# Small inputs in one load, a threshold search shared by two engines, and final norms in five steps: the Hyena and mixture-of-experts trunk on one core

## The chip, the core and the metric

The kernel runs on one core of a Trainium2 chip. The metric is device time of one execution in microseconds, as the median over timed runs. One more execution was recorded by the hardware profiler; the rows below are of that one. Engines are named as in the profile: PE does matrix multiplies, DVE, ACT and POOL work elementwise, SP only issues transfers (DMAs), and ACT and POOL can issue them too.

## The reference, cut to what matters

One layer over 2048 tokens of width 1024. A modulation vector comes from `silu(c) @ mod_w + mod_b`, the tokens are normalised and modulated, a Hyena mixer follows (input projection, a centred 3-tap convolution, two long convolutions whose filters are computed from sines, output projection), then a norm, a second modulation, an expert-choice mixture of experts and a last norm.

```python
x = x + grid_pos_embed(rows, D_MODEL)
m_l = split(silu(c) @ mod_w[i] + mod_b[i], 6)
hl = layer_norm(x) * (1.0 + m_l[1]) + m_l[0]
yl = hyena(hl, ...)              # filters: sin(freq * (z @ f_w1 + f_b1)), twice more with f_w2, f_b2
x = ln_affine(ALPHA * x + (1.0 + m_l[2]) * yl, ln_g[i, 0], ln_b[i, 0])
hl = layer_norm(x) * (1.0 + m_l[4]) + m_l[3]
aff = softmax(hl @ w_router)                       # 2048 x 16
gate, idx = top_k(aff.T, 256)                      # each of 16 experts takes its 256 best tokens
he = silu(xe @ w1) * (xe @ w3)                     # xe = hl[idx], 256 x 1024; w1, w3: 1024 x 2048
ye = (he @ w2) * gate                              # w2: 2048 x 1024
x = ln_affine(ALPHA * x + (1.0 + m_l[5]) * scatter_add(ye), ln_g[i, 1], ln_b[i, 1])
```

## The kernel before, in words

Matrix products of 32-bit floats are made of halves: a tile is cast by ACT to a rounded high part (`wh`, `hh`, `w1h`), and DVE subtracts it from the original to give the low part (`wl`, `hl`, `w1l`). Two or three products of parts make one full product.

**Start.** Three strands run together. `early_mod` loads 16 pieces of `mod_w` (tile `mw`, five buffers, issued by SP) and multiplies them by `sg`, partly on PE, partly on DVE into `macc` (L464, L467); PE then sums over partitions into `sd` (L470), and `md` (L473) is the modulation. `filter_acts` makes the filters' sines: PE multiplies, ACT scales (`turn`, L211), DVE reduces to one turn (`kk`, L213 and L214), ACT takes the sine (L215). `side_steps` normalises the tokens in quarters of four tiles: POOL adds the position terms (L496, L497), DVE takes statistics (`bst`, `stat`), `rstd_steps` turns variance into 1/sqrt (`lva`, `lsq`, `r`, `nb`; L383 to L392), ACT applies it (L506), PE transposes, ACT applies `md` (`ht`, L526), and the input projection (`ip`) begins. Small parameters come in transfers of their own: `cs` and `mb` by SP, `fb` in six by ACT (L193 to L195), `prm` in three by ACT (L593 to L595), the latter gathered four bytes at a time. A scheduler sets the order of instructions on each engine here.

**Route.** After the output projection the router's logits `lg` go through a softmax. `phase_route` finds each expert's 256th largest score by a search over the bits of its value, two bits in a step, 15 steps: DVE counts scores at or above three candidates (three instructions at L1320, with a sum kept by each), PE adds the counts over the partitions of an expert (`cp`, L1322), DVE counts how many candidates have 256 or more (`ge`, L1338) and makes the next candidates (`cand`, L1342; the partial threshold `thr` at L1328 and the next bases at L1335). Meanwhile the first expert's weights are split: ACT casts and POOL subtracts, six tensors of 128x2048 (`split(raws, nc.gpsimd)`, L1401). `route(0)` then gathers the first expert's 256 tokens by an indirect transfer and transposes them in four steps through one buffer, `tp`.

**Experts.** Sixteen experts in turn, each in eight chunks of 256 hidden columns, each chunk in two halves. A half is `project` (w1 and w3 products), `hidden` (silu times the other, `u`, then `hh` and `hl`) and `back` (product with w2 into `acc`, one half later). Weights of a later chunk are cast by ACT (L1400) and split by DVE (L1401); SP issues their loads in order.

**The last three experts** are written in an order by hand, 16 steps (`n`) of one half each. Between their steps `settle` does the last norm of the tokens, 256 at a time. It is a generator of which one step runs in each half: load; nothing; statistics and, right behind them, 1/sqrt by three Newton steps in tiny POOL operations (L1565 to L1577); then ACT's scaling of `xs` (L1580) and POOL's `gb` multiply and add (L1581, L1582) and the store. `plan` says at which step of which expert a settle starts, ten in all here. The buffers `free` of the settles belong to the pair that also holds the experts' gathered tokens, so `route(e + 1)` writes its `xs` (L1484) into a buffer that a settle used.

## Time and profile before

| | us |
|---|---|
| median of 3 runs | 4089.68 (4086.54 to 4090.18) |
| the profiled execution, its own time | 4085.04 |
| its span, first to last instruction | 4083.2 |
| PE busy | 3833.0 (94%) |
| DVE / ACT / POOL busy | 2789.9 / 1940.8 / 1040.3 |
| from the end of the search to the experts' first product | 1827.80 to 1846.77 |

The span is the time that the rows of the trace add up to; 1.84 us lie around it. The profiled execution is 4.64 us below the median of the runs shown.

### The profile page before, as it was taken

What the parts mean: (1) busy time and instruction counts of PE and PEld (TensorE: products, weight loads), DVE (VectorE), ACT (ScalarE), POOL (GpSimd) and SP (SyncE); (2) the same over time, 40 slices, a digit from 0 to 9 for tenths busy, and PEclk for the clock granted to TensorE, in tenths of its full rate; (3) what the DMA queues carried; (4) which work ended last, traced back from release to release, by engine and by line L of the source; (5) the groups of instructions that cost most, each with busy time, mean ns of one, the idle gap of its engine ahead of it and who ended that gap; (6) DMA issues with size and microseconds to landing.
All of it is one profiled execution on the core that took longest, in us unless ns stands there. A gap on an engine that the chain in (4) does not pass through costs nothing.

```text
span 4083.2 us, 52931 instructions
## 1 busy us (share of the span) xinstructions
PE 3833.0 (94%) x19839; PEld 3171.7 (78%) x19839; DVE 2789.9 (68%) x4017; ACT 1940.8 (48%) x2845; POOL 1040.3 (25%) x1092
## 2 busy tenths in 40 slices
PE   4899999999999989939999999999999999999997
PEld 3666766777777877827888888888888888888896
DVE  5777876776877877785666666666666666656766
ACT  3544543333777651114555555555555555544443
POOL 2355552212455442220000000000000000014635
PEclk8999999999999999969999999999999999999999
DMA  6355656667999986445666665666566656656764
GB/s 201 113 175 173 179 172 210 221 205 227 268 283 278 294 251 203 136 162 167 196 193 209 206 196 188 214 204 195 188 215 203 195 189 213 203 176 221 238 228 159
DMA packets 620796, 831.73 MB, mean 204 GB/s; under 512 B 56627, under 2 KB 506947, under 8 KB 618236
## 3 DMA queue, kind: packets, MB, share of 16 engines
q1 hardware_dynamic: 545594, 661.93, 50.8%
q0 software_dynamic: 57088, 163.48, 13.7%
q10 hardware_dynamic: 17858, 2.95, 0.5%
q8 instruction: 156, 2.56, 0.3%
q14 instruction: 100, 0.82, 0.1%
HBM read 643.82 MB, written 150.75 MB: 195 GB/s over the span
## 4 chain that ended last, share of the span: by engine, by line
PE 75%; DVE 9%; issue 5%; DMA 4%; POOL 3%; ACT 3%; SPq 0%; ACTq 0%; POOLq 0%; DVEq 0%
PE ab L1502 19%; PE ab L1503 10%; PE acc L175 5%; PE acc L176 5%; PE acc L177 5%; PE ip L175 3%; PE ip L177 3%; PE ip L176 3%; PE sp L335 2%; PE xp L854 2%; PE ap L889 2%; PE xp L872 2%; PE op L175 1%; PE op L177 1%; PE op L176 1%
## 5 line engine op out<-in xcount | busy, mean ns | idle before, releaser
L1502 PE MATMUL ab<-xs,w3h 128*128 128x512 f32 x1664 | 600.6, 399 | 0.0
L1502 PE MATMUL ab<-xs,w1h 128*128 128x512 f32 x1664 | 598.2, 399 | 0.0
L1401 DVE TENSOR_TENSOR w2l<-w2r,w2h 128x2048 fp32r<-128x2048 f32 x126 | 297.6, 2362 | 267.0 <-ACT w2h L1400 266.9
L1503 PE MATMUL ab<-xs,w3l 128*128 128x256 f32 x1664 | 468.2, 281 | 0.0
L1503 PE MATMUL ab<-xs,w1l 128*128 128x256 f32 x1664 | 466.6, 280 | 0.0
L175 PE MATMUL acc<-w2h,hh 128*128 128x512 f32 x1024 | 404.1, 395 | 14.3 <-ACT hh L170 13.8
L176 PE MATMUL acc<-w2l,hh 128*128 128x512 f32 x1024 | 402.5, 393 | 0.0
L177 PE MATMUL acc<-w2h,hl 128*128 128x512 f32 x1024 | 399.5, 391 | 0.8 <-DVE hl L171 0.8
L1502 PEld LDWEIGHTS ab<-xs,w3h 128*128 128x128 f32 x1664 | 313.0, 188 | 76.6
L1502 PEld LDWEIGHTS ab<-xs,w1h 128*128 128x128 f32 x1664 | 313.0, 188 | 72.9
L1548 POOL DMA_INDIRECT accd<-y,idx x27 | 68.5, 2535 | 1101.8 <-DVE y L1542 1095.6
L1401 DVE TENSOR_TENSOR w1l<-w1r,w1h 128x2048 fp32r<-128x2048 f32 x126 | 301.0, 2389 | 62.7 <-ACT w1h L1400 62.6
L170 ACT CAST hh<-u 128x256 fp32r<-128x256 f32 x256 | 104.1, 407 | 478.6 <-DVE u L1525 478.6
L1503 PEld LDWEIGHTS ab<-xs,w1l 128*128 128x128 f32 x1664 | 314.2, 189 | 7.1
L1506 DVE TENSOR_TENSOR u<-ab,u 128x256 f32<-128x256 f32 x416 | 174.6, 420 | 205.2 <-ACT u L1505 196.8
L1503 PEld LDWEIGHTS ab<-xs,w3l 128*128 128x128 f32 x1664 | 314.8, 189 | 0.0
L1401 DVE TENSOR_TENSOR w3l<-w3r,w3h 128x2048 fp32r<-128x2048 f32 x126 | 292.9, 2324 | 18.7 <-ACT w3h L1400 18.7
L1400 ACT CAST w2h<-w2r 128x2048 fp32r<-128x2048 f32 x128 | 244.1, 1907 | 94.7 <-PE acc L177 86.3
L1400 ACT CAST w1h<-w1r 128x2048 fp32r<-128x2048 f32 x128 | 244.5, 1910 | 80.5 <-PE ab L1502 79.0
L1400 ACT CAST w3h<-w3r 128x2048 fp32r<-128x2048 f32 x128 | 244.5, 1910 | 68.4 <-PE ab L1502 66.3
L1505 ACT COPY u<-ab 128x256 f32<-128x256 f32 x416 | 152.8, 367 | 184.9 <-PE ab L1503 184.8
L175 PE MATMUL ip<-hh,wh 128*128 128x512 f32 x576 | 237.4, 412 | 3.3 <-ACT hh L170 3.3
(399 smaller groups left out, 9114.7 us busy)
## 6 DMA issues: line engine op xcount, KB each, us to landing
w1r<-in_moe_w_dram SPq DMA_DIRECT2D x128, 1024.0 KB
w3r<-in_moe_w_dram SPq DMA_DIRECT2D x128, 1024.0 KB
w2r<-in_moe_w_dram SPq DMA_DIRECT2D x128, 1024.0 KB
fud<-ev SPq DMA_DIRECT2D x128, 256.0 KB
kr<-fud SPq DMA_DIRECT2D x64, 512.0 KB
bn<-ao POOLq DMA_DIRECT2D x248, 128.0 KB, 7.2
win<-in_c_win_dram SPq DMA_DIRECT2D x64, 256.0 KB
mw<-in_mod_w_dram SPq DMA_DIRECT2D x64, 256.0 KB
```

The source lines that it names most:

```text
L170: nc.scalar.copy(hi, raw)
L175: nc.tensor.matmul(out, lhsT=ah, rhs=bh, start=start, stop=False)
L176: nc.tensor.matmul(out, lhsT=ah, rhs=bl, start=False, stop=False)
L177: nc.tensor.matmul(out, lhsT=al, rhs=bh, start=False, stop=stop)
L335: nc.tensor.matmul(p, lhsT=s1[:, th], rhs=hb[th], start=True, stop=(n0 > 0))
L854: nc.tensor.matmul(p[:, i], lhsT=s2[:, 2 * gp + i], rhs=r[:, i], start=True, stop=True)
L1400: nc.scalar.copy(h, raw)
L1401: eng.tensor_tensor(l, raw, f_(h), OP.subtract)
L1502: nc.tensor.matmul(p, lhsT=ws[2 * j][:, k, fs], rhs=xs[:, k], start=(k == 0), stop=False)
L1503: nc.tensor.matmul(p[:, 0], lhsT=ws[2 * j + 1][:, k, fs], rhs=xs[:, k, 0], start=False, stop=(k == 7))
L1505: nc.scalar.copy(u, p[:, 1])
L1506: nc.vector.tensor_tensor(u, p[:, 0], u, OP.add)
```

## The change

Seven parts, in the order in which they run.

1. Seven small inputs are packed by the host into one array of 128x148, which one SP transfer loads into `small`; `cs`, `mb`, `fb` and `prm` become slices of it, and their eleven transfers go.
2. `rstd_steps` takes the square root straight from the variance with the epsilon as ACT's bias, without the DVE addition `lva`; the five DVE operations before `nb` become four. `kk`'s subtraction is written with another instruction, one for one.
3. At the end of the output projection the exponential's table is loaded, and the casts of the first two weight tensors are issued, ahead of the last logits.
4. In the search, DVE counts two candidates and ACT the third (a sign with a kept sum); PE adds them in two products, and `ge` compares with a row of limits `lim`.
5. POOL no longer splits the first expert's weights: DVE does, w1 and w3 of chunk 0 before the search, w2 of chunk 0 and the weights of chunk 1 behind `route(0)`.
6. `route(0, wide=True)` transposes through the projection's buffers `ab` too, and its order is now fixed by hand.
7. `settle` yields once more, between the statistics and the Newton steps, and one settle of the third-last expert starts one half later.

The diff, cut to its core:

```diff
+def host_small(x):
+
+
+    col = lambda v: np.asarray(v, dtype=np.float32).reshape(-1, 128).T
+    two = lambda v: np.concatenate([np.asarray(v, dtype=np.float32).reshape(-1, 64).T] * 2, 0)
+    return np.ascontiguousarray(np.concatenate(
+        [col(x["c"][0]), col(x["mod_b"][0, 0:2048]), col(x["hy_conv_w"][0]), col(x["hy_conv_b"][0]), col(x["hy_b_in"][0]),
+         two(x["hy_f_freq"][0]), two(x["hy_f_b1"][0]), two(x["hy_f_b2"][0])], 1))
...
     nc.scalar.dma_start(fw[0][33:66, 64:128], A["hy_f_w1"][0])
-    for s in range(2):
-        sl = slice(s * 64, s * 64 + 64)
-        nc.scalar.dma_start(fb[sl, 0:1], A["hy_f_freq"][0].unsqueeze(1))
-        nc.scalar.dma_start(fb[sl, 1:2], A["hy_f_b1"][0].unsqueeze(1))
-        nc.scalar.dma_start(fb[sl, 2:4], A["hy_f_b2"][0].rearrange("i k -> k i"))
     nc.scalar.dma_start(zt[:, 0:1024], A["c_z"][:, 0:1024])
...
-        nc.vector.tensor_tensor(kk, turn, kk, OP.subtract)
+        nc.vector.scalar_tensor_tensor(kk, kk, -1.0, turn, op0=OP.mult, op1=OP.add)
...
 def rstd_steps(nc, wk, r, nb, stat, eps, n):
 
-    va = wk.tile([128, n], F32, name="lva")
-    nc.vector.tensor_scalar(va, stat[:, :, 1], eps, None, op0=OP.add)
+    nc.scalar.activation(r, stat[:, :, 1], AF.Sqrt, bias=eps)
+    yield 1
     sq = wk.tile([128, n], F32, name="lsq")
-    nc.scalar.activation(sq, va, AF.Sqrt)
-    yield 1
-    nc.vector.reciprocal(r, sq)
-    nc.vector.tensor_tensor(sq, r, r, OP.mult)
-    nc.vector.tensor_tensor(sq, sq, va, OP.mult)
-    nc.vector.tensor_scalar(sq, sq, -0.5, 1.5, op0=OP.mult, op1=OP.add)
-    nc.vector.tensor_tensor(r, r, sq, OP.mult)
+    nc.vector.reciprocal(r, r)
+    nc.vector.scalar_tensor_tensor(sq, stat[:, :, 1], eps, r, op0=OP.add, op1=OP.mult)
+    nc.vector.scalar_tensor_tensor(sq, sq, -0.5, r, op0=OP.mult, op1=OP.mult)
+    nc.vector.scalar_tensor_tensor(r, sq, 1.5, r, op0=OP.add, op1=OP.mult)
     nc.vector.scalar_tensor_tensor(nb, stat[:, :, 0], -1.0, r, op0=OP.mult, op1=OP.mult)
...
-        prm = S.top.tile([128, 5, 24], F32, name="prm")
-        nc.scalar.dma_start(prm[:, 0:3], A["hy_conv_w"][0].rearrange("j (k p) -> p j k", p=128))
-        nc.scalar.dma_start(prm[:, 3], A["hy_conv_b"][0].rearrange("(k p) -> p k", p=128))
-        nc.scalar.dma_start(prm[:, 4], A["hy_b_in"][0].rearrange("(k p) -> p k", p=128))
+        prm = S.small[:, 24:144].rearrange("p (j k) -> p j k", j=5)
...
-            if n == 16:
+            if n == 17:
+                nc.scalar.activation(wk.tile([128, 1], F32, name="r"), ident[:, 0:1], AF.Exp)
                 next(nxt)
...
+        lim = wk.tile([128, 3], F32, name="lim")
+        nc.gpsimd.memset(lim[:, 0:2], T - CAP + 0.5)
+        nc.gpsimd.memset(lim[:, 2:3], T - 2.0 * CAP + 1.0)
...
-                cnt = wk.tile([128, 3], BF16, name="cnt", bufs=2)
-                for k in range(3):
+                cnt = wk.tile([128, 2], BF16, name="cnt", bufs=2)
+                cs = wk.tile([128, 1], BF16, name="cs", bufs=2)
+                sign = wk.tile([128, 256], BF16, name="sign")
+                with nc.allow_low_precision(reason="whole numbers of at most 256"):
+                    nc.scalar.activation(sign, v, AF.Sign, scale=-1.0, bias=cand[:, 2:3], accum_out=cs)
+                for k in range(2):
                     junk = wk.tile([128, 256], U16, name=f"junk{k}")
-                    nc.vector.tensor_scalar(junk, v, cand[:, k:k + 1], 0.0, op0=OP.is_ge, op1=OP.add, accum_out=cnt[:, k:k + 1])
+                    nc.vector.tensor_scalar(junk, v, cand[:, k:k + 1], 0.0, op0=OP.is_lt, op1=OP.add, accum_out=cnt[:, k:k + 1])
                 p = ps.tile([128, 3], F32, name="cp", bufs=2)
-                nc.tensor.matmul(p, lhsT=blkb, rhs=cnt, start=True, stop=True)
+                nc.tensor.matmul(p[:, 2:3], lhsT=blkb, rhs=cs, start=True, stop=True)
+                nc.tensor.matmul(p[:, 0:2], lhsT=blkb, rhs=cnt, start=True, stop=True)
...
-                nc.vector.tensor_scalar(ge, p, CAP - 0.5, 0.0, op0=OP.is_ge, op1=OP.add, accum_out=num)
+                nc.vector.scalar_tensor_tensor(ge, p, 1.0, lim, op0=OP.mult, op1=OP.is_le, accum_out=num)
...
+    hs = [(n, raw, wt.tile(list(raw.shape), F32R, name=n + "h"), wt.tile(list(raw.shape), F32R, name=n + "l")) for n, raw in raws]
+
+    def sub(i):
+        _, raw, h, l = hs[i]
+        nc.vector.scalar_tensor_tensor(l, raw, 1.0, f_(h), op0=OP.mult, op1=OP.subtract)
+
+    for i in range(2):
+        nc.scalar.copy(hs[i][2], hs[i][1])
+    for i in range(2):
+        sub(i)
     nc.vector.tensor_scalar(R.tri, ii, 128.0, None, op0=OP.is_gt)
     nc.vector.tensor_scalar(ii, ii, 15, None, op0=OP.bitwise_and)
     nc.vector.tensor_scalar(R.blkb, ii, 0.0, None, op0=OP.is_equal)
+    R.first = [t for h in hs for t in h[2:]]
     yield
-    R.first = []
-    for n in range(2):
-        R.first.append(split(raws, nc.gpsimd))
-        if n == 0:
-            raws = load(0, 1)
+    nc.scalar.copy(hs[2][2], hs[2][1])
+    yield
+    sub(2)
+    raws = load(0, 1)
+    R.second = split(raws[:2])
+    R.raw = raws[2:]
...
-                p = ps.tile([128, 2, 256], F32, name="tp", bufs=1)
+                p = ps.tile([128, 2, 256], F32, name="ab", bufs=3) if wide and q else ps.tile([128, 2, 256], F32, name="tp", bufs=1)
...
             for j in range(2):
                 ln_stats(nc, wk, stat, j, x[:, j])
+            yield
             va = wk.tile([128, 2], F32, name="va2")
...
-        with tc.manual_schedule():
-            for _ in route(0):
-                pass
+        first = route(0, wide=True)
+        next(first)
+        next(R.split_first)
+        next(first)
+        for _ in first:
+            pass
+        next(R.split_first)
+        order.close()
...
-        plan = {-3: {1: "xh", 3: "xl", 5: "xh"}, -2: {0: "xh", 2: "-xl", 5: "xh"}, -1: {0: "xh", 2: "-xl", 5: "xh", 7: "xl"}}
+        plan = {-3: {1: "xh", 3: "xl", 6: "xh"}, -2: {0: "xh", 2: "-xl", 5: "xh"}, -1: {0: "xh", 2: "-xl", 5: "xh", 7: "xl"}}
...
+            S.small = S.top.tile([128, 148], F32, name="small")
+            nc.sync.dma_start(S.small, A["c_small"])
```

ACT at the start of the program, from the last small filter weights to the first sines; `prm` is the convolution's and input projection's parameters, `a` a sine. Before:

```order
L201 DMA fw_121<-in_hy_f_w_dram 64x64 x2
L211 ACTIVATE turn<-sp,frq 128x512
L211 ACTIVATE turn<-g,frq 128x512
L211 ACTIVATE turn<-sp,frq 128x512
L593 DMA prm<-in_hy_conv_w_dram 128x72x1
L594 DMA prm<-in_hy_conv_b_dram 128x24x1
L595 DMA prm<-in_hy_b_in_dram 128x24x1
L215 ACTIVATE a_459<-kk 128x512 x2
L211 ACTIVATE turn<-g,frq 128x512
L211 ACTIVATE turn<-sp,frq 128x512
L215 ACTIVATE a_459<-kk 128x512
```

And after the change:

```order
L205 DMA fw_118<-in_hy_f_w_dram 64x64 x2
L215 ACTIVATE turn<-sp,frq 128x512
L215 ACTIVATE turn<-g,frq 128x512
L215 ACTIVATE turn<-sp,frq 128x512
L219 ACTIVATE a_446<-kk 128x512
L215 ACTIVATE turn<-g,frq 128x512
L219 ACTIVATE a_446<-kk 128x512
L215 ACTIVATE turn<-sp,frq 128x512
L219 ACTIVATE a_446<-kk 128x512
```

The three `prm` transfers that stood between the third `turn` and the first sine are gone, and the sines alternate with the `turn`s from there on.

DVE in one step of the search (`half` is the 16-bit half of a score that is searched, `junk` a result that nobody reads, `kc` the table of first candidates). Before:

```order
L1320 TENSOR_SCALAR junk_15099,cnt<-half_15094,kc 128x256
L1320 TENSOR_SCALAR junk_15101,cnt<-half_15094,kc 128x256
L1320 TENSOR_SCALAR junk_15103,cnt<-half_15094,kc 128x256
L1324 MEMSET thr_15097 128x1
L1326 COPY half_15093<-afp 128x256
L1335 TENSOR_SCALAR base<-kc,thr_15097 128x3
L1338 TENSOR_SCALAR ge,num<-cp 128x3
L1342 SCALAR_TENSOR_TENSOR cand<-num,base 128x3
L1320 TENSOR_SCALAR junk_15117,cnt<-half_15094,cand 128x256
```

After the change, on DVE:

```order
L1321 TENSOR_SCALAR junk_15062,cnt<-half_15054,kc 128x256
L1321 TENSOR_SCALAR junk_15064,cnt<-half_15054,kc 128x256
L1326 MEMSET thr_15057 128x1
L1328 COPY half_15053<-afp 128x256
L1337 TENSOR_SCALAR base<-kc,thr_15057 128x3
L1340 SCALAR_TENSOR_TENSOR ge,num<-cp,lim 128x3
L1344 SCALAR_TENSOR_TENSOR cand<-num,base 128x3
L1321 TENSOR_SCALAR junk_15082,cnt<-half_15054,cand 128x256
```

And on ACT, from the first weight casts to the end of the search (`sign` is the result that nobody reads, `cs` the kept sum):

```order
L1437 CAST w1h<-w1r 128x2048
L1437 CAST w3h<-w3r 128x2048
L1235 COPY lg<-rp 128x32
L1218 COPY ht<-tp 128x4x128 x2
L1228 COPY lp<-rp 128x256
L1235 COPY lg<-rp 128x32
L1285 ACTIVATE lg<-lg 128x256
L1318 ACTIVATE sign,cs<-half_15054,kc 128x256
L1318 ACTIVATE sign,cs<-half_15054,cand 128x256 x6
L1318 ACTIVATE sign,cs<-half_15053,kc 128x256
L1318 ACTIVATE sign,cs<-half_15053,cand 128x256 x7
L1445 CAST w2h<-w2r 128x2048
```

One count of three has moved to ACT; ahead of the softmax ACT now casts `w1h` and `w3h`, which stood behind it, and `w2h` comes behind the search.

DVE in the second-last expert, around one settle's statistics (`bst`, `stat` of `xs`) and the first small operations of its Newton steps (`va`, `t`, `r`). Before:

```order
L1401 TENSOR_TENSOR w1l<-w1r,w1h 128x2048
L1401 TENSOR_TENSOR w3l<-w3r,w3h 128x2048
L376 BN_STATS bst<-xs 128x6 x2
L377 BN_AGGR stat_32000<-bst 128x2
L376 BN_STATS bst<-xs 128x6 x2
L377 BN_AGGR stat_32000<-bst 128x2
L1565 TENSOR_SCALAR va_32009<-stat_32000 128x2
L1569 TENSOR_SCALAR t_32013<-va_32009 128x2
L1570 TENSOR_SCALAR r_32011<-t_32013 128x2
L1454 TENSOR_SCALAR oh<-slot,lo 128x256
L1455 SCALAR_TENSOR_TENSOR oh<-slot,hi,oh 128x256
```

After the change:

```order
L380 BN_STATS bst<-xs 128x6 x2
L381 BN_AGGR stat_32000<-bst 128x2
L380 BN_STATS bst<-xs 128x6 x2
L381 BN_AGGR stat_32000<-bst 128x2
L1469 TENSOR_SCALAR oh<-slot,lo 128x256
L1470 SCALAR_TENSOR_TENSOR oh<-slot,hi,oh 128x256
L1540 TENSOR_TENSOR u_32068<-u_32068,ab 128x256
L181 TENSOR_TENSOR hl<-u_32068,hh 128x256
L1403 TENSOR_TENSOR w2l<-w2r,w2h 128x2048
L1581 TENSOR_SCALAR va_32093<-stat_32000 128x2
L1585 TENSOR_SCALAR t_32097<-va_32093 128x2
L1586 TENSOR_SCALAR r_32095<-t_32097 128x2
```

`va` has moved from right behind the statistics to the end of the next half, behind that half's split `w2l`.

## Rows read from the trace of the kernel before

**Rows 1.** Windows: length, busy PE, PEld, DVE, ACT, POOL; PE clock, DMA share, GB/s.

```profile
0.00:115.00 115.00, 57.52 (x206) 40.77 (x207) 64.30 (x118) 48.71 (x73) 26.45 (x32) 0.82 0.62 179
115.00:680.00 565.00, 529.13 (x2356) 381.43 (x2356) 424.18 (x527) 272.77 (x468) 300.54 (x248) 0.98 0.56 169
...
1776.28:1827.80 51.52, 2.46 (x15) 1.46 (x14) 49.59 (x170) 8.64 (x5) 26.24 (x6) 0.50 0.50 162
...
1846.77:3630.00 1783.23, 1782.68 (x9470) 1520.15 (x9469) 1120.91 (x1401) 915.76 (x1198) 89.16 (x50) 1.00 0.62 197
3630.00:4063.00 433.00, 414.08 (x2871) 384.79 (x2870) 284.03 (x299) 189.33 (x194) 217.21 (x208) 0.99 0.66 219
```

**Rows 2.** Chain that ended last, the first 140 us: start, us, what.

```profile
25.60 0.80 ACTq L594
26.39 14.44 issue
...
56.78 7.00 PE sd L470 x32
```

**Rows 3.** Windows of 5 us at the start, columns as in rows 1.

```profile
40.00:45.00 5.00, 1.31 (x2) 0.80 (x3) 0.14 (x1) 1.81 (x3) 0.00 (x0) 1.00 0.55 6
```

**Rows 4.** DMA queues, first 60 us: packets, MB, share of 16 engines.

```profile
q10 hardware_dynamic: 16738, 0.72, 19.3%
```

**Rows 5.** Timeline at the start, DVE, POOL and PE: start, us, what.

```profile
44.85 0.43 DVE L213 TENSOR_SCALAR kk<-turn 128x512 f32<-128x512 f32 x1 [14.15 <-ACT turn L211]
63.80 0.24 DVE L473 SCALAR_TENSOR_TENSOR md<-sd,mb 128x8 f32<-128x8 f32 x2 [4.62 <-PE sd L470]
67.02 8.04 DVE L383 TENSOR_SCALAR lva<-stat 128x4 f32<-128x4 f32 x1
67.69 1.27 POOL L496 TENSOR_TENSOR x<-x,pr 128x512 f32<-128x512 f32 x1
80.31 0.15 DVE L392 SCALAR_TENSOR_TENSOR nb<-stat,r 128x4 f32<-128x4 f32 x1
98.53 0.79 PE L175 MATMUL ip<-x,wh 128*128 128x512 f32 x1 [7.49 <-ACT ht L526]
```

**Rows 6.** DVE groups in the search: xcount, busy us, mean ns, idle before.

```profile
L1320 DVE TENSOR_SCALAR_CACHE_REDUCE junk<-half,cand 128x256 uint16<-128x256 uint16 x39 | 16.6, 476 | 0.5
L1342 DVE SCALAR_TENSOR_TENSOR cand<-num,base 128x3 f32<-128x3 f32 x13 | 10.5, 806 | 0.5
```

**Rows 7.** Timeline of the route and the first expert.

```profile
1773.43 0.40 ACT L1287 ACTIVATE lg<-lg 128x256 f32<-128x256 f32 x1
1775.71 4.52 POOL L1401 TENSOR_TENSOR w1l<-w1r,w1h 128x2048 fp32r<-128x2048 f32 x1 [43.18 <-ACT w1h L1400]
1805.34 0.48 DVE L1320 TENSOR_SCALAR_CACHE_REDUCE junk<-half,cand 128x256 uint16<-128x256 uint16 x1
1807.29 0.48 DVE L1320 TENSOR_SCALAR_CACHE_REDUCE junk<-half,cand 128x256 uint16<-128x256 uint16 x1
1859.44 2.29 DVE L1401 TENSOR_TENSOR w1l<-w1r,w1h 128x2048 fp32r<-128x2048 f32 x1 [1.55 <-ACT w1h L1400]
```

**Rows 8.** Waits in the last experts: who for whom, total us, times, longest.

```profile
PE acc L175 <- ACT hh L170: 13.8, 8, 3.3
ACT xs L1580 <- POOL nb L1577: 38.0, 10, 6.0
ACT xs L1484 <- DMA out_dram<-xs: 4.0, 2, 2.2
SPq L1555 <- DMA out_dram<-xs: 8.9, 1, 8.9
```

**Rows 9.** Timeline of one settle in the third-last expert.

```profile
3700.74 1.27 DVE L376 BATCH_NORM_STATS2 bst<-xs 128x6 f32<-128x512 f32 x2
3703.69 1.90 DVE L1565 TENSOR_SCALAR va<-stat 128x2 f32<-128x2 f32 x1
3716.39 2.37 ACT L1580 ACTIVATE xs<-xs,nb,r 128x1024 f32<-128x1024 f32 x2 [6.02 <-POOL nb L1577]
```

More of the change, by code (lines that the diff above doesn't have):

```diff
@@ L177, in mm3, with filter_acts @@
     nc.tensor.matmul(out, lhsT=al, rhs=bh, start=False, stop=stop)
-def filter_acts(tc, A, ld, ps, afw, arv):
+def filter_acts(tc, A, fb, ld, ps, afw, arv):
     nc = tc.nc
-    fb = ld.tile([128, 4], F32, name="fb")
     zt = ld.tile([128, T], F32, name="zt")[0:66]
@@ L439, in late_mod, with early_mod @@
         yield
-def early_mod(nc, A, md, sg, ones_f, wk, ps):
-    cs = wk.tile([128, 8], F32, name="cs", bufs=1)
-    nc.sync.dma_start(cs, A["c"][0].rearrange("(k p) -> p k", p=128))
+def early_mod(nc, A, cs, mb, md, sg, ones_f, wk, ps):
     nc.scalar.activation(sg, cs, AF.Silu)
-    mb = wk.tile([128, 2, 8], F32, name="mb", bufs=1)
-    nc.sync.dma_start(mb, A["mod_b"][0, 0:2048].rearrange("(i k p) -> p i k", i=2, p=128))
     yield
@@ L503, in norm @@
         nb = wk.tile([128, 4], F32, name="nb")
-        yield from rstd_steps(nc, wk, r, nb, stat, ADALN_EPS, 4)
+        yield from rstd_steps(nc, wk, r, nb, stat, eps, 4)
         for j in range(4):
@@ L537, in side_steps @@
         pr = wk.tile([128, 512], F32, name="pr", bufs=1)
+        eps = wk.tile([128, 1], F32, name="eps", bufs=1)
+        nc.vector.memset(eps, ADALN_EPS)
         nc.gpsimd.dma_start(pr, A["c_posr"])
@@ L1287, in phase_route @@
         nc.scalar.activation(lg, lg, AF.Exp)
-        next(R.split_first)
         nc.vector.tensor_reduce(mx, lg, axis=mybir.AxisListType.X, op=OP.add)
@@ L1443, in phase_moe @@
     with ExitStack() as st:
-        with tc.manual_schedule():
-            phase_route(tc, ident, ones_f, lg, R)
+        order = st.enter_context(ExitStack())
+        order.enter_context(tc.manual_schedule())
+        phase_route(tc, ident, ones_f, lg, R)
         cst = st.enter_context(tc.tile_pool(reuse_waits="tile", name="e_cst", bufs=1))
@@ L1449, in phase_moe, with route @@
         ps = st.enter_context(tc.tile_pool(reuse_waits="tile", name="e_ps", bufs=2, space=PSUM))
-        def route(e):
+        def route(e, wide=False):
             oh = wk.tile([128, 256], F32, name="oh", bufs=1)
@@ L1588, in phase_moe @@
         nxt, pend = [], []
-        with tc.manual_schedule():
-            for _ in route(0):
-                pass
+        first = route(0, wide=True)
[6 more added lines that the diff above has]
+        order.close()
         m5 = cst.tile([128, 1024], F32, name="m5")
@@ L1605, in phase_moe @@
             for fc in range(8):
-                ws = R.first.pop(0) if R.first else R.split(R.load(e, fc))
+                if e == 0 and fc < 2:
+                    ws = (R.second + R.split(R.raw)) if fc else R.first
+                else:
+                    ws = R.split(R.load(e, fc))
                 for i in range(2):
@@ L1753, in build @@
                         tc.tile_pool(reuse_waits="tile", name="m_wk", bufs=2, side="right") as mk:
-                    mod = early_mod(nc, A, md, sg, ones_f, mk, sps)
+                    mod = early_mod(nc, A, S.small[:, 0:8], S.small[:, 8:24].rearrange("p (i k) -> p i k", i=2), md, sg, ones_f, mk, sps)
                     next(mod)
-                    acts = filter_acts(tc, A, ld, fps, afw, arv)
+                    acts = filter_acts(tc, A, S.small[:, 144:148], ld, fps, afw, arv)
                     side = side_steps(tc, A, md, ident, S, psum, h2d)
@@ L1800 @@
     given.update(host_consts())
+    given["c_small"] = host_small(given)
+    for n in ("c", "hy_conv_w", "hy_conv_b", "hy_b_in", "hy_f_freq", "hy_f_b1", "hy_f_b2"):
+        del given[n]
     for n, a in given.items():
```

4 lines of the change are left out of this document (1 added, 3 removed).

## Prediction

> **What bounds the kernel now.** Read first the windows by stage [rows 1]. From 1846.77 to 3630 PE is busy for 1782.68 of 1783.23 us: nothing that another engine does there can shorten the kernel, and whatever ends the stages before it sooner is kept. From 115 to 680 PE is busy for 529 of 565 us, so a shift that reaches the input projection is mostly handed on. Three stretches are not PE's: the first 115 us (57.52 busy), the threshold search (2.46 busy in 51.52 us, DVE 49.59) and the last three experts (414.08 of 433.00, so 18.9 us of holes). The change touches these three.
>
> Next, the start. The chain of waits [rows 2] shows ACT at L594 from 25.60, then 14.44 us under "issue", then PE's sums `sd` at 56.78. ACT issues the small `prm` transfers in the same order in which it computes sines, so DVE, which wants ACT's `turn` for `kk` at 44.85, stands idle for 14.15 us [rows 5], and DVE's multiplications of `mw` stand behind that `kk`. SP has five `mw` buffers; in 40 to 45 us the DMA engines are 0.55 busy but move 6 GB/s [rows 3], which is the small pieces: one queue with 16738 packets for 0.72 MB takes 19.3% of 16 engines over 60 us, 11.6 us of all of them [rows 4]. `md` comes at 63.80. A second stall follows: the four-element `lva` takes 8.04 us while POOL's additions run (67.69 and on), and `nb` is issued at 80.31, the first `ip` product at 98.53 [rows 5].
>
> In the search, a step that nothing disturbs takes 1.95 us (counts start at 1805.34 and 1807.29 [rows 7]); 15 such steps would be 29.3 us, and the search takes 51.5. The rest is in tiny operations: `cand`, three elements, has a mean of 806 ns, while the 256-wide counts stay at 476 [rows 6]. POOL's subtractions, 4.52 us each, begin at 1775.71 [rows 7], six of them.
>
> In the last experts the list of waits [rows 8] puts 13.8 us of PE's holes on `hh`, and 38.0 us of ACT's own on `nb`, POOL's last Newton operation, ten times. In the settle of [rows 9] the statistics start at 3700.74, `va` behind them at 3703.69, and ACT waits 6.02 us before it scales at 3716.39; its next `u` and `hh`, for which PE waits, stand behind.
>
> **The change part by part.**
>
> *Start.* Gone are the `prm` and `fb` transfers. The 14.44 us on ACT go, and the 11.6 us of DMA time that overlap them; `md` moves by 14.4 at least if data keep up, by about 20 if `mw` then flows without a hole. I take 18. The `lva` addition goes (8.04 us, normally 0.16 as the size of `nb`'s 0.15 shows): but the same quarter's new operations still run near POOL's additions, so of 7.9 I take 4. Together 22 us at the first `ip`. Lower bound 12: the ACT stall alone, less 2.4 for data that arrive no sooner. Upper: 20 + 8 + 2 for sines that are also ready sooner, 30. The four operations in place of five save 0.15 us a quarter, nothing that shows.
>
> *Search.* DVE then counts twice and ACT once beside it. The nearest row for ACT is the 256-wide exponential, 0.40 us [rows 7], against two counts of some 0.40 each (three fill 1.95 less 0.75 of small operations): ACT is hidden if its kept sum costs less than 0.4 more. The trace has no such ACT operation. Below, the step falls by a whole count, to 1.55; above, ACT's path is as long as the third count and it stays 1.95. The row is nearest to the first; 15 x 1.55 and 1.05 for the extra copies make 24.3 in place of 51.5: 27.2 gained, or 21.2 at the upper bound. The extra product on PE and the load of `lim` lie in PE's idle time (2.46 us busy). DVE's `w1l` and `w3l`, 2.29 each [rows 7], now precede the softmax, where DVE waited for logits; ACT's two casts ahead of the last logits put the start back by some 0.7 us, with the earlier table load counted. 26.5.
>
> *Behind the route.* Three splits that POOL made during the search, and one more soon after, now stand in DVE's queue before `u`: 4 x 2.29 = 9.2 us, of which PE's first products cover most (the first half's products end some 12 us after 1846.77, before the split of [rows 7] at 1859.44). I take 2.5 us of hole; bounds 0 (all covered) and 6 (two splits uncovered, with the queue behind). Transposes at once and no longer between products: PE does the same number, nothing. Net of search and this: -24, bounds -17 (21.2 less 4) and -30.
>
> *Settles.* `va` leaves the tail of the statistics for the end of the next half, and ACT's scaling moves by one half (8.5 us) too. What is won is the statistics' own time, 2.95 us (3703.69 - 3700.74), between the last split and `va`: the ten waits, 3.8 on average, would fall to about 1, and PE's 13.8 us to about 5. That is 8 to 9 us. Against it, `out` stores end one half later (for the moved settle, two), and ACT's `xs` of the next expert and SP's reloads wait for them already (4.0 in two, and 8.9 us [rows 8]); I give 2 back. Net -7; at best all of 13.8, -14; at worst the stores cost 6 more than the waits give, +6. Where POOL meets DVE, `va` stretches to 1.90 [rows 9]; that can fall on the new place as well, inside the bounds.
>
> *Sum.* -22 - 24 - 7 = -53. The profiled execution has 4085.04, so 4032.0; it stands 4.64 below the median of the runs, 4089.68, and against the median the sum gives 4036.7. I say 4037. The two kernels can be told apart by about 0.2%, 8 us.
>
> **The rivals.**
>
> A. *The start gives most of it back.* POOL's additions of the second quarter now start sooner as well, so they lie over the new square-root operations or over `wl`, and a small operation waits 8 us there as `lva` did (8.04 [rows 5]) and `wl` another 2 to 4. For it: both are chains of the same loads. Against: if `mw` lands sooner, `x` of the second quarter does too, and may be done before `nb`. Only some 10 of 22 us stay: 4049. The Trainium skill (SBUF — State Buffer, "SBUF: two separate sides") says that DVE and POOL share a pair of ports which is locked for a whole instruction, and that a DVE operation with two inputs in SBUF takes part in it when POOL reads SBUF. By that rule the new three-operand instructions are no better than `lva`, and the gain of that part would be 0 instead of 4; the trace agrees in so far as `lva` lasted 8.04 us over POOL's rows.
>
> B. *ACT's count isn't hidden*, and the splits behind the route hold PE: step 1.95 (+6), hole 6 (+3.5). For it: no row shows ACT with a kept sum, and the candidate must reach ACT as well as DVE. Against: 0.40 beside two counts. 4046.
>
> C. *Settles no faster or slower.* The stores that end later hold ACT's `xs` casts for the next expert and SP's weight loads behind its reloads. For it: the 8.9 and 4.0 us. Against: one settle in each expert is near enough. +8 instead of -7: 4052.
>
> D. *Slower than before.* One mechanism: SP's queue. A reload of a settle's buffer waits for a later store, and all weight loads behind it wait as well, once in each of the ten settles. It turns the result when the last three experts lose more than 46 + 8 = 54 us, or 5.4 us of PE per settle, on top of what is there: the hold must then exceed the lead of the loads by that much each time. One hold of 8.9 us has cost nothing on PE's list so far (weights account for 3.6 us there at most, by 18.9 less 13.8 and rests). 4100.
>
> E. *The change doesn't do what it says:* ACT's stall at L594 was the DMA engines' and not `prm`'s, and merely moves to the next transfer, with the start unchanged; 4059. Against: that transfer's 4-byte pieces are the only such queue.
>
> **How the numbers follow.** Chances: the forecast 0.50, A 0.20, B 0.13, C 0.10, D 0.03, E 0.04. The forecast's own range, from the terms' bounds taken as independent (10, 7 and 13 us on the bad side, 8, 6 and 7 on the good), is 4025 to 4052. The range of 4021 to 4058 leaves out D, E and the joint of two rivals on one side, and two good ends together on the other. Faster by over 0.2%: all but D and parts of E with C, 0.95; within 0.2%: 0.02; slower: 0.03.
>
> **What the changed profile would show.** The chain of the start without "issue" near 26 us, `md` near 46, first `ip` near 76. The search in 24 to 25 us with DVE steps of 1.55, POOL idle, `cand` at 0.16. PE with a hole of 2 to 3 us around the first `acc`. In the list of waits of the last experts ACT for `nb` near 10 us, PE for `hh` near 5, and in their place a few more us of ACT for `out` stores. The prediction is wrong if a small DVE operation of several us still stands before the first `ip`, if the sign lasts longer than two counts, or if PE's holes behind 3630 sum to over 18.9.

## The result, and the profile after

The changed kernel takes 4054.27 us (median of 4 runs, 4053.97 to 4058.61) against 4089.93 for the kernel before: ratio 0.9915, interval 0.9898 to 0.9932, that is 28 to 42 us faster. The forecast was 4037, with a range to 4058: the direction held, a third of the forecast gain didn't come. The profiled execution took 4053.97, its span 4052.0. One execution of the kernel before, 5105.97 us at a granted clock of 0.704, is left out of every median and ratio below.

The windows of the changed kernel, at the places that answer to [rows 1] (the start, the search, the way to the experts, thirteen experts, the last three):

```profile
0.00:97.00 97.00, 57.34 (x204) 40.90 (x205) 67.25 (x115) 49.64 (x73) 28.59 (x32) 0.77 0.62 212
1763.65:1789.05 25.40, 4.89 (x30) 3.02 (x29) 22.72 (x140) 9.91 (x31) 0.00 (x0) 0.50 0.45 142
1789.05:1808.83 19.78, 6.99 (x30) 6.19 (x30) 8.89 (x31) 3.15 (x5) 2.16 (x2) 0.50 0.40 133
1808.83:3590.00 1781.17, 1781.17 (x9463) 1519.28 (x9464) 1129.25 (x1404) 919.47 (x1199) 90.08 (x51) 1.00 0.62 200
3590.00:4031.80 441.80, 412.42 (x2865) 384.79 (x2864) 283.79 (x298) 190.08 (x194) 211.00 (x208) 0.98 0.64 215
```

The search has halved, 51.5 to 25.4 us, POOL is idle in it, and from the first expert's first product on PE never stops. The way from the search to that product takes 19.8 us, where it took 19.0. And the last three experts have grown holes: 441.80 - 412.42 = 29.4 us against 18.9 before.

To see where the time went, the start of the same PE instruction was taken in both traces, and the difference (median over the instructions of a stretch) set against its time in the kernel before:

```
stretch of before, us    sooner by, us
first ip product           16.8   (98.53 -> 81.73)
150 to 250                 18.2
500 to 680                 15.1
950 to 1000                 9.5
1100 to 1450               13.1
1550 to 1750 (op)          13.4
1846.77, first expert      37.9   (1846.77 -> 1808.83)
3000 to 3690               40.8
3750 to 3800               29.1
end                        31.2
```

So the start gave 17 to 18 us at the input projection and 13.4 behind the output projection; the route 24.5 up to the first expert and 27.4 with the first experts; and the last experts took 9.6 back.

Timeline rows of the start of the changed kernel, DVE, POOL, ACT and PE, in answer to [rows 5]:

```profile
19.68 2.89 DVE L217 TENSOR_SCALAR kk<-turn 128x512 f32<-128x512 f32 x2
22.49 3.42 DVE L218 SCALAR_TENSOR_TENSOR kk<-kk,turn 128x512 f32<-128x512 f32 x2
50.65 0.24 DVE L470 SCALAR_TENSOR_TENSOR md<-sd,small 128x8 f32<-128x8 f32 x2 [5.07 <-PE sd L467]
55.78 5.55 DVE L390 SCALAR_TENSOR_TENSOR lsq<-stat,eps,r 128x4 f32<-128x4 f32 x1
56.39 1.27 POOL L493 TENSOR_TENSOR x<-x,pr 128x512 f32<-128x512 f32 x1
60.05 1.25 POOL L494 TENSOR_TENSOR x<-x,pc 128x512 f32<-128x512 f32 x1
63.00 0.15 DVE L393 SCALAR_TENSOR_TENSOR nb<-stat,r 128x4 f32<-128x4 f32 x1
81.73 0.80 PE L185 MATMUL ip<-x,wh 128*128 128x512 f32 x1 [7.04 <-ACT ht L523]
```

And its windows of 5 us there, columns as in [rows 3]:

```profile
25.00:30.00 5.00, 5.00 (x19) 2.82 (x19) 5.00 (x7) 2.83 (x5) 2.03 (x2) 1.00 0.73 269
30.00:35.00 5.00, 5.00 (x27) 3.33 (x27) 5.00 (x8) 3.82 (x7) 0.00 (x0) 1.00 0.78 254
35.00:40.00 5.00, 4.17 (x10) 1.52 (x8) 5.00 (x8) 1.88 (x3) 0.00 (x0) 1.00 0.84 259
```

ACT's long stall is gone, and DVE is now the busy engine: 5.00 of 5.00 us in each window, while the DMA engines move 254 to 269 GB/s. `md` comes 13.2 us sooner. The stall of `lva` has not gone: another four-element operation, `lsq`, lasts 5.55 us over POOL's additions. In both kernels the stalled operation ends 0.03 us behind the last of POOL's additions, and not behind the first: `lsq` at 61.33 behind four of them, `lva` before the change at 75.06 behind six, of which this is the last:

```profile
73.78 1.25 POOL L497 TENSOR_TENSOR x<-x,pc 128x512 f32<-128x512 f32 x1
```

So the stall is 2.5 us shorter because fewer additions were left, by these rows, and not because the operation is another.

The lists of waits in the last experts, PE, ACT and SP, in answer to [rows 8]:

```profile
PE tp L1497 <- DVE xs L1500: 18.4, 2, 15.4
PE ab L187 <- DVE w3l L1403: 5.1, 4, 1.3
PE ab L187 <- DVE w1l L1403: 3.7, 4, 1.6
PE acc L185 <- ACT hh L180: 1.8, 3, 0.7
...
ACT xs L1596 <- POOL nb L1593: 31.8, 9, 5.9
ACT xs L1499 <- DMA out_dram<-xs: 21.4, 2, 16.6
...
SPq L1570 <- DMA out_dram<-xs: 25.6, 3, 16.8
```

The wait for `hh` fell from 13.8 to 1.8 us, further than forecast, though ACT's wait for `nb` fell only from 38.0 to 31.8. Two others have grown. PE's wait for the split `w3l` was smaller before:

```profile
PE ab L177 <- DVE w3l L1401: 0.5, 2, 0.2
```

And one wait that was not on the list of these experts before is the largest now: PE stands 15.4 us in the third-last expert for the next expert's transposes, behind DVE's and ACT's halves of `xs`, and ACT stands 16.6 us for a store of a settle.

The place itself, POOL's store and ACT's cast, first in the kernel before, then in the changed kernel:

```profile
3729.92 0.63 POOL L1586 DMA_DIRECT2D out_dram<-xs  x1 [0.30 <-POOL xs L1582]
3738.71 0.59 ACT L1484 CAST xs<-tp 128x512 fp32r<-128x512 f32 x1 [2.15 <-DMA out_dram<-xs]
```

```profile
3700.65 0.62 POOL L1602 DMA_DIRECT2D out_dram<-xs  x1 [0.30 <-POOL xs L1598]
3709.29 0.59 ACT L1499 CAST xs<-tp 128x512 fp32r<-128x512 f32 x1 [16.64 <-DMA out_dram<-xs]
```

Before, the third settle's store was issued 6.6 us ahead of the moment at which ACT reached the cast (3736.56), and the buffer came free 8.8 us behind the issue. In the changed kernel ACT reached the cast at 3692.65, the store was issued only at 3700.65, 8.0 us behind that, and released the buffer 8.6 us later. Against ACT the store is 14.6 us later, and that is the growth of the wait, from 2.15 to 16.64. All of ACT's work behind that cast stood too.

### The profile page after: what moved, and what is told of

The parts are those of the page before. It is cut to its first block, busy times and chain, and to the rows that moved or that the text cites. A ratio compares the mean times of both kernels' runs of the same rounds, so it can differ in the third digit from the quotient of the medians.

```text
span 4052.0 us, 52976 instructions
## 1 busy us (share of the span) xinstructions
PE 3837.7 (95%) x19854; PEld 3179.1 (78%) x19854; DVE 2779.6 (69%) x3986; ACT 1951.6 (48%) x2875; POOL 1011.0 (25%) x1088
## 3 DMA queue, kind: packets, MB, share of 16 engines
q0 software_dynamic: 57088, 163.48, 13.8%
## 4 chain that ended last, share of the span: by engine, by line
PE 74%; DVE 7%; DMA 6%; issue 5%; POOL 4%; ACT 3%; SPq 0%; POOLq 0%; ACTq 0%; DVEq 0%
PE ab L1517 19%; PE ab L1518 10%; PE acc L185 5%; PE acc L186 5%; PE acc L187 5%; PE ip L185 3%; PE ip L187 3%; PE ip L186 3%; PE xp L850 2%; PE ap L885 2%; PE xp L868 2%; PE sp L339 1%; PE op L185 1%; PE op L187 1%; PE op L186 1%
## 5 line engine op out<-in xcount | busy, mean ns | idle before, releaser
L1403 DVE TENSOR_TENSOR w3l<-w3r,w3h 128x2048 fp32r<-128x2048 f32 x127 | 301.8, 2376 | 18.8 <-ACT w3h L1402 18.8
```

Source lines behind the costliest of these rows:

```text
L1403: eng.tensor_tensor(l, raw, f_(h), OP.subtract)
```

## The experiments

The medians of one kernel, taken again, lie some 3 us apart (4054.27 and 4057.39 for the changed one), its single executions up to 18, so the last experts were judged by the holes of their traces, and the times by the medians with their intervals. Times in brackets are ranges.

**The settles as before, in the changed kernel.**

```diff
                 ln_stats(nc, wk, stat, j, x[:, j])
-            yield
...
-        plan = {-3: {1: "xh", 3: "xl", 6: "xh"}, ...
+        plan = {-3: {1: "xh", 3: "xl", 5: "xh"}, ...
```

> The changed kernel with the settles as before: four steps, the third settle of the third-last expert at step 5. Theory (the five steps and the later start make the last experts slower, since ACT's cast of the next expert's tokens waits 16.6 us for a store and PE 15.4 us behind it): the last experts win back the 9.7 us that they lost, 4054.3 becomes 4044 to 4045, the wait of ACT for a store falls from 21.4 to about 4 us, that for POOL's nb rises from 31.8 to about 38. Rival (what was lost behind 3600 is noise of the weight loads or a port collision that the search's new place brought along): the time stays at 4052 to 4056.

4043.41 us (4038.52 to 4046.72), ratio 0.9895 (0.9878 to 0.9911). PE's and ACT's lists of waits:

```profile
PE acc L185 <- ACT hh L180: 11.9, 8, 2.8
...
ACT xs L1595 <- POOL nb L1592: 38.0, 10, 6.0
ACT xs L1499 <- DMA out_dram<-xs: 4.7, 2, 3.0
```

The holes for `hh` and the wait for `nb` are back at the size of before, the wait for the store is small, and the kernel is 11 us faster than the whole change by the medians, 8 by the ratios to the kernel before. No execution of the one is as slow as the fastest of the other. The settles' part does harm.

**The two halves of that part, one at a time.** Five steps with the third settle at step 5, and four steps with it at step 6:

```diff
-        plan = {-3: {1: "xh", 3: "xl", 6: "xh"}, ...
+        plan = {-3: {1: "xh", 3: "xl", 5: "xh"}, ...
```

> The changed kernel with five steps, but the third settle of the third-last expert back at step 5. Theory (the stall's size is the store's lateness): the store ends one half, 8.5 us, sooner, so PE's hole of 15.4 falls to about 7 and the time to about 4046. Rival (a reload that starts sooner waits at SP for the first settle's store, and the weight loads behind it are late): the hole goes, but SP's wait for stores rises by 8 us and PE waits for weights instead, 4052 to 4058.

4044.75 us (4039.48 to 4049.95). PE waited 6.1 us for transposes in two places, 3.0 at most, ACT 9.6 us for stores in two, and SP's longest wait for a store was 20.1 us without a hole of that size on PE: the rival's weights were not late.

```diff
                 ln_stats(nc, wk, stat, j, x[:, j])
-            yield
```

> The changed kernel with four steps, and the third settle of the third-last expert at step 6 as in the change. Theory: the store is one half late in place of two, ACT's wait about 8 to 9 us, PE's hole about 7, time 4050 to 4052, since PE's holes for hh come back as well. Rival (the moved start does no harm, only the fifth step does): as x1, 4044 to 4045.

4045.69 us (4045.32 to 4049.29). One hole for transposes, 3.0 us.

Timeline rows of the third settle's store and of ACT's cast: with neither delay (the run above), with five steps at 5, and with four steps at 6.

```profile
3688.32 0.63 POOL L1601 DMA_DIRECT2D out_dram<-xs  x1 [0.30 <-POOL xs L1597]
3697.90 0.59 ACT L1499 CAST xs<-tp 128x512 fp32r<-128x512 f32 x1 [2.95 <-DMA out_dram<-xs]
```

```profile
3697.89 0.62 POOL L1602 DMA_DIRECT2D out_dram<-xs  x1 [0.30 <-POOL xs L1598]
3702.67 0.58 ACT L1499 CAST xs<-tp 128x512 fp32r<-128x512 f32 x1 [4.77 <-DMA out_dram<-xs]
```

```profile
3694.59 0.63 POOL L1601 DMA_DIRECT2D out_dram<-xs  x1 [0.30 <-POOL xs L1597]
3699.36 0.58 ACT L1499 CAST xs<-tp 128x512 fp32r<-128x512 f32 x1 [4.75 <-DMA out_dram<-xs]
```

I expected 7 us of hole for each, half of the whole. Each alone makes 3, both together 15.4. The lateness does add up: the store is issued 6.6 us ahead of the moment at which ACT reaches the cast with neither delay, at that moment with either one, and 8.0 us behind it with both. What differs is how long the buffer stays taken behind the issue: 9.6 us with neither, 4.8 with each alone, 8.6 with both. SP's loads of weights go with it. The last one ahead of the store, in the changed kernel and with five steps at 5:

```profile
3696.70 0.57 SPq L1393 DMA_DIRECT2D w3r<-in_moe_w_dram  x1
```

```profile
3682.32 0.53 SPq L1393 DMA_DIRECT2D w3r<-in_moe_w_dram  x1
```

In the changed kernel three loads of 1 MB were issued 4 to 5 us ahead of the store, and the DMA engines moved 336 GB/s until the buffer came free; with neither delay it was much the same, 4 to 5 us and 300 GB/s. With each delay alone the last load lay 15.6 us ahead, and they moved 266 and 258 GB/s. So each alone seems to have been cheap partly because the loads ahead of its store were done; no run moves the loads by themselves.

**The fifth step and the later start alone, on the kernel before.** The diff is the settles' part of the change and nothing else.

```diff
                 ln_stats(nc, wk, stat, j, x[:, j])
+            yield
...
-        plan = {-3: {1: "xh", 3: "xl", 5: "xh"}, ...
+        plan = {-3: {1: "xh", 3: "xl", 6: "xh"}, ...
```

> The kernel before with the fifth step of the settles and the moved start alone. Theory (this part by itself makes the kernel slower): the last experts lose 9 to 10 us, PE waits some 15 us in the third-last expert for the transposed tokens, 4089 becomes 4098 to 4100. Rival (it gains the 7 us that the prediction gave it, and only together with the other parts it does harm): 4080 to 4083.

4100.36 us (4092.96 to 4103.09) against 4088.38, ratio 1.0025 (1.0015 to 1.0034), slower by 6 to 14 us. Its list of PE's waits has the lines of the changed kernel, the first one but for 0.2 us:

```profile
PE tp L1482 <- DVE xs L1485: 18.6, 2, 15.6
PE ab L177 <- DVE w3l L1401: 5.1, 4, 1.3
...
PE acc L175 <- ACT hh L170: 1.8, 3, 0.7
```

**The settle moved where no expert follows.** Five steps kept; the third settle of the third-last expert runs in the last expert.

```diff
-        plan = {-3: {1: "xh", 3: "xl", 6: "xh"}, -2: {0: "xh", 2: "-xl", 5: "xh"}, -1: {0: "xh", 2: "-xl", 5: "xh", 7: "xl"}}
+        plan = {-3: {1: "xh", 3: "xl"}, -2: {0: "xh", 2: "-xl", 5: "xh"}, -1: {0: "xh", 2: "-xl", 5: "xh", 7: "xl", 11: "xh"}}
```

> The changed kernel with five steps, and the third settle of the third-last expert moved into the last expert, at step 11, where no next expert wants the buffer and no weight load stands behind its reload. Theory: the hole of 15.4 us goes and nothing takes its place; the settles' steps spaced out then show their gain (hh 13.8 to 1.8 us): 4054.3 - 15 = 4039, plus 0 to 4 if the last settle's store or POOL's work runs into the tail: 4039 to 4043. Rival (the last expert has no room for a fifth settle): its scaling and store end behind the last product, the tail grows by about 10 us, and the time is 4048 or more.

4043.65 us (4041.18 to 4046.54); the profiled execution 4041.18. PE's holes fall to 14 us and its last product ends 18 us sooner than in the changed kernel, but the tail behind it grows from 19.3 us (4032.7 to 4052.0) to 24.9 (4014.5 to 4039.4): POOL's last scaling runs into it. Theory and rival are both seen, each with its own price. Set against the settles as before, whose last product ends 10 us sooner than in the changed kernel, five steps without the hole are worth 8 us at the last product, and the longer tail takes most of that: the two medians are the same. POOL's timeline at that place:

```profile
4024.03 0.59 POOL L1602 DMA_DIRECT2D out_dram<-xs  x1 [0.30 <-POOL xs L1598]
4024.64 2.37 POOL L1720 TENSOR_TENSOR xs<-xs,xg 128x1024 f32<-128x1024 f32 x1
```

The tail's own POOL operation (L1720) starts as soon as that store is issued, with no idle time before it.

**Four steps where something follows, five elsewhere.** That settle, and the third of the second-last expert, take four steps (`four` skips the new `yield`).

```diff
-            yield
+            if not four:
+                yield
...
+        plan = {-3: {1: "xh", 3: "xl"}, -2: {0: "xh", 2: "-xl", 5: "+xh"}, -1: {0: "xh", 2: "-xl", 5: "xh", 7: "xl", 11: "+xh"}}
```

> The changed kernel with five steps, but the third settle of the third-last expert moved into the last expert at step 11, and that one and the third of the second-last expert in four steps. Theory (a settle that ends in front of a cast of the next expert, or of the tail, must end sooner; the others gain by five steps): PE's holes behind 3600 sum to 11 to 13 us, the tail is 20 us long again, time 4035 to 4039. Rival (four steps there bring the holes for hh back): 4041 to 4045.

4044.80 us (4037.45 to 4050.08), the profiled execution 4037.45 with a span of 4034.9. Its tail is 20.4 us long (4014.5 to 4034.9) and no PE wait for transposes is left, but holes for `hh` come back:

```profile
PE acc L185 <- ACT hh L180: 8.8, 5, 5.8
```

From the first expert to the last product it gains 15.8 us on the changed kernel in the aligned traces; in the medians it can't be told from the four others at 4043 to 4046. All beat both kernels; which of them is best stays open.

**The start alone, on the kernel before** (`small`, the square root and `kk`, as in the diff of the change).

```diff
+            S.small = S.top.tile([128, 148], F32, name="small")
+            nc.sync.dma_start(S.small, A["c_small"])
...
+    nc.scalar.activation(r, stat[:, :, 1], AF.Sqrt, bias=eps)
```

> The kernel before with the parts of the start alone: the packed small inputs, the square root without lva, and kk's other instruction. Theory (the start is worth what the aligned traces show, 18 us at the first products of the input projection and 13 behind the output projection): 4089 becomes 4072 to 4077. Rival A (most of it is given back): 4079 or more. Rival E (the stall of ACT merely moves): 4086 or more.

4074.48 us (4067.85 to 4078.33) against 4089.10, ratio 0.9964 (0.9952 to 0.9976): 10 to 20 us. In its aligned trace the first products are 18 us sooner and those of the experts 17. What `fb`'s transfers and what `prm`'s are worth by themselves was not tried.

**The old square root in the changed kernel** (and the old instruction of `kk`).

```diff
-    nc.scalar.activation(r, stat[:, :, 1], AF.Sqrt, bias=eps)
+    nc.vector.tensor_scalar(va, stat[:, :, 1], eps, None, op0=OP.add)
+    nc.scalar.activation(sq, va, AF.Sqrt)
```

> The changed kernel with the square root and kk as before: lva back, seven small operations. Theory of the prediction (the new root is worth 4 us at the first ip): the first ip comes 3 to 5 us later than in the changed kernel, lva lasts about 8 us over POOL's additions. Rival (the stall has only moved from lva to lsq, 5.55 us in the changed kernel, and depends on where POOL's additions stand): the first ip within 2 us of the changed kernel's 81.73, the whole within 4 us of 4054.

4056.86 us (4054.39 to 4059.81). DVE's timeline:

```profile
53.53 0.15 DVE L387 TENSOR_SCALAR lva<-stat 128x4 f32<-128x4 f32 x1
56.06 4.95 DVE L392 TENSOR_TENSOR lsq<-r 128x4 f32<-128x4 f32 x1
```

The first `ip` is at 81.58, 0.15 sooner than in the changed kernel. `lva` is short here, and the product after it takes the stall. The new root is worth nothing at this place: the operation that meets POOL's additions stands, until 61.01, 0.03 us behind the last of them.

**The route alone, on the kernel before** (parts 3 to 6 of the change).

```diff
-    R.first = []
-    for n in range(2):
-        R.first.append(split(raws, nc.gpsimd))
...
+                    nc.scalar.activation(sign, v, AF.Sign, scale=-1.0, bias=cand[:, 2:3], accum_out=cs)
```

> The kernel before with the parts of the route alone: the casts ahead of the last logits, the count on ACT, the splits on DVE and the transposes through ab. Theory (27 us, of which 26 lie in the search): 4089 becomes 4060 to 4064, the search takes 25 to 26 us. Rival B (the splits behind the route hold PE by some 6 us): 4066 to 4069.

4061.29 us (4053.62 to 4067.67), ratio 0.9934 (0.9917 to 0.9951): 20 to 34 us. By the medians the three parts give 14.6, 27.8 and -12.0 us, together 30.4; the whole gave 35.7, and 31.0 when it was run again. They add up within what the intervals leave.

**Three counts on DVE, in the changed kernel.**

```diff
-                    nc.scalar.activation(sign, v, AF.Sign, scale=-1.0, bias=cand[:, 2:3], accum_out=cs)
-                for k in range(2):
+                for k in range(3):
```

> The changed kernel with all three counts on DVE, POOL still idle in the search. Theory (the search lost 20 us to POOL's subtractions and 6 to the third count): steps of 1.95 us, the search about 31 us in place of 25.4, the first expert's first product 5 to 6 us later than in the changed kernel, the whole about 4060. Rival (the count on ACT was the longer way, and the search is won by POOL's absence alone): the search within 1 us of 25.4.

4061.76 us (4060.18 to 4064.71). The search takes 30.62 us (1767.20 to 1797.82) in place of 25.40: the count on ACT is worth 5.2 us, and POOL's absence the rest, 51.5 - 30.6 = 20.9.

**POOL's subtractions put back beside the changed kernel's search.** The six write the same low parts once more.

```diff
+    R.again = lambda: [nc.gpsimd.tensor_tensor(hs[i][3], hs[i][1], f_(hs[i][2]), OP.subtract) for i in (0, 1) * 3]
...
         nc.gpsimd.memset(lim[:, 2:3], T - 2.0 * CAP + 1.0)
+        R.again()
```

> The changed kernel with six POOL subtractions of 128x2048 put back beside the search; they write the low parts of w1 and w3 once more with the same values. Theory (POOL's subtraction stops DVE's tiny operations with operands in SBUF): the search grows from 25.4 to 40 to 47 us, cand, thr and base last 3 to 4.5 us several times, the two 256-wide counts stay at 0.48. Rival (the search was slow before since its operations were written otherwise): it stays within 2 us of 25.4.

4082.77 us in one execution. They came to stand ahead of the search, over the softmax, so the search itself stayed at 25.4 us, where I had expected the loss; its start moved by 22 us past what the stages before account for. DVE's timeline there, POOL's six running from 1764.36 to 1791.67:

```profile
1764.57 4.40 DVE L1443 TENSOR_SCALAR ii<-ii 128x128 int32<-128x128 int32 x1
1769.01 4.42 DVE L1444 TENSOR_SCALAR blkb<-ii 128x128 bf16<-128x128 int32 x1
1773.35 0.41 DVE L1284 TENSOR_REDUCE mx<-lg 128x16 f32<-128x256 f32 x1
1773.79 4.29 DVE L1285 TENSOR_TENSOR lg<-lg,mx 128x256 f32<-128x256 f32 x1
```

In the changed kernel the same `ii`, `blkb` and `lg` take 0.23, 0.23 and 0.42 us; the reduction takes 0.42 there and 0.41 here. The price of POOL's work beside DVE's small operations is shown, 22 us for six, in that one execution.

**The changed kernel once more.**

> The changed kernel once more, beside the others. Both theories: 4054 within 5 us. The place of the same instruction in two profiled executions shows how far the stages before the route move by themselves: if by 4 us and more, the difference of 5 us between the first ip (18 us sooner) and the output projection (13 sooner) needs no cause in the change; if by under 1, it does.

4057.39 us (4056.44 to 4060.51), ratio 0.9928 (0.9912 to 0.9945). Against the first trace the same instructions lie up to 2.5 us off in the stages ahead of the route, between the two bounds that were set, so this run alone decides nothing. Six other kernels here have the same program up to the end of the output projection (the four settle variants, the mixed steps and the three counts). At its products these seven traces lie between 4.5 us sooner and 3.6 us later than the first one of the changed kernel, so a difference of 5 us there needs no cause in the change.

## Why the prediction was right or wrong

**Sum.** -22 - 24 - 7 = -53 was forecast; the aligned traces give -13.4 - 27.4 + 9.6 = -31.2. That the time lies inside the stated range is in part luck: the settles left their own bounds of -14 to +6, and what the route gave beyond its -24 covered a part of it. The forecast's own range was also added up too short: 10, 7 and 13 us taken as independent are 18, so it ends at 4055 and not at 4052. Of the three signs of being wrong two came, the small DVE operation of several us (`lsq`) and the holes over 18.9 (29.4).

**Settles: the sign was wrong, and this is the step that failed.** The failing step is the sentence "I give 2 back" for stores that end later. It took its price from the waits of before (4.0 in two), as if a wait would grow by a small share, where it had to count the new end of the third settle: one half for the fifth step and one for the later start, 17 us, against a cast that waited 2.2 us already. The trace shows the store 14.6 us later against ACT, 16.6 us of ACT's wait and 15.4 of PE's. That is rival C, of which the place was right and the price, "+8 instead of -7", nearly so (+9.6). The experiments show the cause: with the part undone the hole goes and 11 us come back; alone on the kernel before it costs 6 to 14.

The other side of the term came, but not all by the way that it named. PE's waits for `hh` went from 13.8 to 1.8 us, better than the "about 5", while ACT's waits for `nb`, which were to fall near 10, stayed at 31.8. In the kernel before, one of the holes stands behind DVE's `u`, which comes behind `va` and two more small operations:

```profile
3705.90 0.41 DVE L1525 TENSOR_TENSOR u<-u,ab 128x256 f32<-128x256 f32 x1
3706.81 0.50 PE L175 MATMUL acc<-w2h,hh 128*128 128x512 f32 x1 [2.07 <-ACT hh L170]
```

In the changed kernel `u` follows the statistics at once, and `va` comes 5 us later. No run tells how much of the 12 us each way gave. And a cost stands beside it that the term did not have: with the settles moved, POOL's `gb` operations lie over DVE's split `w3l` five times, where they did so twice. There the split takes 4.5 us in place of 2.3, and at four of the five PE waits for it, 5.1 us in all. One of them beside POOL's addition:

```profile
3666.73 4.47 DVE L1403 TENSOR_TENSOR w3l<-w3r,w3h 128x2048 fp32r<-128x2048 f32 x1
3669.13 4.33 POOL L1598 TENSOR_TENSOR xs<-xs,gb 128x1024 f32<-128x1024 f32 x1
```

**Start: the mechanism right, two sizes off.** ACT's stall at the `prm` transfers went. `md` was to come 18 us sooner and came 13.2: the term overlooked that DVE, freed from waiting, has the sines' `kk` and the products with `mw` to do in the same 15 us, and is busy throughout (5.00 of 5.00 us in three windows), with its first `kk` pairs at 2.9 and 3.4 us over POOL's additions, where such pairs took 0.75 and 1.29 in the kernel before. The 4 us for the square root were 0, and that is rival A's mechanism at less than its price: `lsq` lasts 5.55 us and not 8, and `wl`, for which A added 2 to 4, keeps its 1.21. The rule cited from the Trainium skill (SBUF — State Buffer, "SBUF: two separate sides"), under which the new three-operand instruction is no better than `lva`, is what the trace shows, except that `lsq` stands for four of POOL's instructions and not for one. At the first `ip` 16.8 of the 22 were there. Of those, 13.4 reach the route in the one pair of traces and 16.3 with the start alone; since programs that are the same so far lie 4.5 us sooner to 3.6 later there, I can't say that the change gives 3 us back in between.

**Route: right, a little low.** The search was to take 24.3 us and takes 25.4. ACT's count is hidden: its 256 elements take 0.51 us and the kept sum another 0.19, and PE's product with ACT's `cs` begins 0.2 us ahead of the one with DVE's counts, which comes 0.05 us behind DVE's last sum (1771.26). Timeline of ACT and PE in one step of the changed kernel's search:

```profile
1770.45 0.51 ACT L1318 ACTIVATE sign<-half,cand 128x256 bf16<-128x256 uint16 x1 [1.01 <-DVE cand L1344]
1770.86 0.19 ACT L1318 ACTIVATION_READ_ACCUMULATOR sign<-half,cand 128x1 bf16 x1
1771.10 0.16 PE L1323 MATMUL cp<-cs,blkb 128*128 128x1 bf16 x1 [1.24 <-ACT sign L1318]
1771.31 0.16 PE L1324 MATMUL cp<-cnt,blkb 128*128 128x2 bf16 x1
```

The 1.1 us too many lie mostly in front of `cand`: in 11 of its 13 steps DVE has one more semaphore instruction there, and such a step takes 1.62 us, where one without it takes 1.54.

The hole of 2.5 us behind the route did not come: PE's first window of the experts has 1781.17 busy of 1781.17. DVE did the three splits right behind the transposes (from 1809.58 to 1816.27), under products that began at 1808.83. Rival B is out on both counts. Between the first product and the later experts another 2.9 us were gained (37.9 to 40.8), which the term put at nothing; no run tells which part gave them.

**D and E.** Loads behind SP's held reloads cost PE nothing that shows: SP waited up to 16.8 and 20.1 us for stores without a hole of PE for weights. E, that ACT's stall merely moves, is out: from 15.72 to 36.88 us, from ACT's first `turn` on, its longest wait in the changed kernel is 3.50 us, and the start alone gives 10 to 20 us.

## What to carry to other kernels

When a step is moved later, follow the buffer that it holds to the next engine that wants it, and count the whole new lateness against that engine's slack; the present size of the wait says nothing, since it is what is left of the slack. When a step is moved to another half, look also at what the other engines do in that half. A stall put on a tiny operation belonged here to the pair of engines, not to the operation: rewriting the operation moved the stall to its neighbour (`lsq`), taking the other engine's work away removed it (the search). When a blocked engine is freed, add up the work that it now has to do before crediting the whole stall.

## What the runs showed of the hardware that was not expected

Which of DVE's operations stand while POOL subtracts. In the rows of the changed kernel with POOL's work put back, integer and float operations of a single tensor stand as well (`ii` 4.40 us for 0.23, the copy `aff` 4.49 for 0.38), a reduction of the same kind of data doesn't (0.41), nor, in [rows 6], do the counts that keep a sum (0.476). The Trainium skill (SBUF — State Buffer, "Who interferes with whom") excepts the form of the scalar operation that writes out its accumulator, and the trace agrees.

How long such an operation stands. At the start it stood until the last of POOL's additions, six of 1.26 us for `lva` (8.04) and four for `lsq` (5.55); with POOL's subtractions each stalled operation stood for one of them only (4.40 of 4.5). No run shows why.

A buffer's release after a store of 1 MB came 4.8 us behind its issue in the two kernels whose last weight load was issued 15.6 us ahead of the store, and 8.4 to 9.6 us behind it in the five (the kernel before, the changed one twice, the settles as before, and five steps alone) where three loads of 1 MB were issued in the 5.2 us ahead of it. No run moves the loads alone, so that they are the cause is not shown.
